# A written TensorE order with overlapping groups, and SiLU as one ScalarE function, in the state space stage of an encoder trunk

## The chip, the cores and the metric

The kernel runs on one core of a Trainium2 chip. The metric is the device time of one execution in microseconds. The kernel before takes 2204.69 us, the median of 3 runs (2203.37 to 2206.54).

## What is computed

Two layers of an encoder trunk, with 512 tokens of width 1024 and 256 memory tokens. Each layer feeds x into three branches: a bidirectional state space branch (SSD), differential attention and cross-attention. Each branch is projected back to 1024 channels and multiplied by a sigmoid gate computed from x; the sum goes through one output projection, the residual and a layer norm. The change is in the SSD branch, of which this is the reference, cut to what matters:

```python
xbc = silu(centred_dwconv(xbc, conv_w, conv_b))      # 5 taps over tokens
xs, bm, cm = split(xbc)       # 32 heads x 64, and 4 groups x 128 for B and for C
dt = softplus(dt_raw + dt_bias); a = -exp(a_log)
y  = scan(xs*dt_f, dt_f*a_f, bm, cm) + flip(scan(flip(...)))  # chunks of 128 tokens
y  = (y + d_skip*xs) * silu(z)
return rmsnorm(y, norm_w)
...
# in scan(): what is within a chunk, and what comes from other chunks
decay  = exp(where(lower, a_cum[q] - a_cum[s], -inf))
y_diag = einsum(cm, bm, decay, xs)
states = einsum(bm, exp(a_cum[-1] - a_cum), xs)       # summed on from chunk to chunk
y_off  = einsum(cm, prev_states, exp(a_cum))
```

## The kernel before: tiles, stages and what sets the order

**Units.** The weights are cut into 336 units of 128x1024 numbers (512 KB). SyncE loads a unit into `wr` (2 buffers), ScalarE copies it rounded to `wh` (3 buffers), and VectorE forms the remainder `wl = wr - wh` (3 buffers). A projection (`proj`, line 166) goes through the 8 slices k of x and makes three matmuls for each, `wl·xh`, `wh·xl`, `wh·xh`: 24 matmuls of 128x512 into one PSUM bank of the pool `pj` (3 banks). The pool `pm` (4 banks) takes the scan's matmuls and `pt` (1 bank) the transposes. `proj2` (line 189) is the same projection as a generator that hands control back after 4 of the 8 slices; before, only the differential attention (`diff`, line 826) uses it.

**The plan.** `T(fn, unit)` (line 128) puts a step on a list. `emit` (line 131) goes through the list, issues the load and the split of units up to two ahead (`look_raw=2, look=2`), and calls the step. A scheduler then places each engine's instructions by priority, which follows the order in which they were issued; `late(n)` (line 100) lowers the priority of what is issued in it, and inside `manual_schedule(engines={PE})` the TensorE order is the written one.

**The SSD stage** (`ssd`, line 446) runs per layer over 4 groups g, each of 4 blocks b of 128 channels (2 heads). In order: `bpart` (457) projects B, runs `conv` (433) and transposes it to `bT`; `cpart` (468) does C and the product of B and C within chunks (`gs`); `dt_tables` (350), in group 0 only, loads `wdt` into the scratch tile `yh`, projects dt, and writes the cumulative sums to DRAM (`dab`, `deb`). In layer 0 the first B and C run side by side (`bcpart`, 482). Then 4 times `xpart` (488: projection, `conv`, four transposes under `late(LX)`, and the copy to `xsT`), `states` (499: for each direction three `xw` on VectorE, each with one matmul into `pm`), and 4 times `zpart` (523) and `ypart` (532). `ypart` loads `eb` and `ab` from `deb` and `dab`, makes two groups of three "far" matmuls, multiplies them into `eb` on VectorE, puts 8 Exp of 128x128 per head over `ab` on ScalarE, forms the two tiles `m` on VectorE, and makes 16 "near" matmuls of `m` and `xsT`; a chain on VectorE and ScalarE then forms `y`, `yh` and `yl`. The output projections `wpart` (589) of group g-1 stand between the `xpart` steps of group g.

**At the end of the stage** come three gate units of branch 0 (`gpart`, 624), the four `wpart` of group 3, and then alternately a gate unit and a `fin` (629), which scales one slice of the branch's output by the norm and the gate. Eight gates of branch 2 are computed in the stage at the places of the table `AHEAD` (line 40) and stored to DRAM (`dgt`, `gate_ahead` at 683).

**SiLU** is x·sigmoid(x) = (x/2)(tanh(x/2)+1). `conv` uses weights halved in advance (`hcw`), so that `acc` holds half of x: ScalarE makes the first tap, VectorE four more (`scalar_tensor_tensor` from PSUM), ScalarE `th = Tanh(acc)`, VectorE `(th+1)*acc`. `zpart` makes `th = Tanh(ps/2)` on ScalarE and `(th+1)*ps` on VectorE. The norm of the branch takes up the factor 2 of z with 4·EPS in place of EPS.

Of the kernel before, what the change touches and what calls it, by code (L numbers as in the profile page):

```python
# [37 lines left out]


AHEAD = {(0, 1): [(2, 0)], (0, 2): [(2, 1)], (0, 3): [(2, 2)], (1, 0): [(2, 3)], (1, 2): [(2, 4)],  # L40
         (2, 0): [(2, 5)], (2, 2): [(2, 6)], (3, 1): [(2, 7)]}
# [14 lines left out]
class Net:  # L56
# [243 lines left out]
    def layer_params(self, l):  # L300
        nc, a = self.nc, self.a
        pr = self.t(self.cp, [P, NP_], "pr", bufs=2)
        nc.sync.dma_start(out=pr, in_=a["pk"][l])
        self.par = pr
        self.hgb = self.t(self.cp, [P, 24], "hgb", bufs=2)
        self.ts(self.hgb, pr[:, PGB:PGB + 24], 0.5, ALU.mult)
        self.hcw = self.t(self.cp, [P, 144], "hcw", bufs=2)
        self.ts(self.hcw, pr[:, PCW:PCW + 144], 0.5, ALU.mult)
# [41 lines left out]
    def dt_tables(self, l):  # L350
# [20 lines left out]
        N = 256  # L371
        ps = self.bank(self.pj, "pj")
# [3 lines left out]
        self.act(xc, ps[:64])  # L376
        pt = self.bank(self.pt, "pt")
# [26 lines left out]
        dtot = self.dtot = self.t(sp, [P, 4, 64], "dtot")  # L404
        pc = self.bank(self.pm, "pm")
        pv = pc.rearrange("p (d c h) -> p d c h", d=4, c=4)
        for d, tri in ((0, self.tf), (1, self.tb)):
            self.mm(pv[:, d], tri, da[:, :, d * 32:(d + 1) * 32])
            self.act(cum[:, :, d * 32:(d + 1) * 32], pv[:, d])
        for d in range(2):  # L410
            self.mm(pv[:, 2 + d], self.ones, da[:, :, d * 32:(d + 1) * 32])
# [9 lines left out]
        self.tt(bi, bi, cum, ALU.subtract)  # L421
        pt = self.bank(self.pt, "pt")
# [10 lines left out]
    def conv(self, ps, ci, out):  # L433
# [9 lines left out]
        self.act(th, acc, AF.Tanh)  # L443
        self.stt(out, th, 1.0, acc, ALU.add, ALU.mult)

    def ssd(self, l):
# [9 lines left out]

        def bpart(g, ps=None):
            def f(wh, wl):
                self.bC = self.t(self.sp, [P, S], "bC")
                self.conv(self.proj(wh, wl) if ps is None else ps, 16 + g, self.bC)  # L460
                pt = self.bank(self.pt, "pt")
                for c in range(4):
                    self.tr(pt[:, c * P:(c + 1) * P], self.bC[:, c * P:(c + 1) * P])
                self.bT = self.t(self.sp, [P, S], "bT")
                self.act(self.bT, pt)
            return f

        def cpart(g, ps=None):
            def f(wh, wl):
                self.cC = self.t(self.sp, [P, S], "cC", bufs=2)  # L470
                self.conv(self.proj(wh, wl) if ps is None else ps, 20 + g, self.cC)
                pg = self.bank(self.pm, "pm")
                for c in range(4):
                    q = slice(c * P, (c + 1) * P)
                    self.mm(pg[:, q], self.bC[:, q], self.cC[:, q])
                self.gs = self.t(self.sp, [P, 4, P], "gs", bufs=2)
                self.act(self.gs, pg.rearrange("p (c q) -> p c q", c=4))
                self.xsT = self.t(self.sp, [P, 4, S], "xsT", bufs=2)
                self.xsC = {}
            return f  # L480

        def bcpart(g):
            def f(*ws):
                for part, w, ps in zip((bpart, cpart), ws, self.proj_side(*ws)):
                    part(g, ps)(*w)
            return f

        def xpart(g, b):
            def f(wh, wl):
                xc = self.xsC[b] = self.t(self.sp, [P, S], f"xsC{b}")  # L490
                self.conv(self.proj(wh, wl), 4 * g + b, xc)
                pt = self.bank(self.pt, "pt")
                with self.late(LX):
                    for c in range(4):
                        self.tr(pt[:, c * P:(c + 1) * P], xc[:, c * P:(c + 1) * P])
                self.act(self.xsT[:, :, b * P:(b + 1) * P], pt.rearrange("p (c e) -> p c e", c=4))
            return f

        def states(g):
            def f():  # L500
                sp = self.sp
                self.prev = {}
                for d, order in ((0, (0, 1, 2)), (1, (3, 2, 1))):
                    hs = slice(d * 32 + g * 8, d * 32 + g * 8 + 8)
                    old = None
                    for c in order:
                        xw = self.t(sp, [P, 8, 64], "xw", bufs=2)
                        self.tt(xw, self.xsT[:, c, :].rearrange("p (h e) -> p h e", h=8),
                                bc(self.wst[:, c, hs, None], [P, 8, 64]), ALU.mult)
                        ps = self.bank(self.pm, "pm")  # L510
                        self.mm(ps, self.bT[:, c * P:(c + 1) * P], xw)
                        pv = self.t(sp, [P, 8, 64], f"prev{d}{c}")
                        psv = ps.rearrange("p (h e) -> p h e", h=8)
                        if old is None:
                            self.act(pv, psv)
                        else:
                            self.tt(pv, old, bc(self.dtot[:, c, hs, None], [P, 8, 64]), ALU.mult)
                            self.tt(pv, pv, psv, ALU.add)
                        old = pv
                        self.prev[d, c + 1 if d == 0 else c - 1] = pv.rearrange("p h e -> p (h e)")  # L520
            return f
# [10 lines left out]
        def ypart(g, b):  # L532
            def f():
                sp = self.sp
                if b == 0:
                    self.yh = self.t(sp, [P, 4, S], "yh", F32R)
                    self.yl = self.t(sp, [P, 4, S], "yl", F32R)

                eb = self.t(sp, [P, 2, S], "eb", bufs=2)
                for hh in range(2):  # L540
                    h = g * 8 + 2 * b + hh
                    src = self.deb.rearrange("(d h) q -> h d q", d=2)[h:h + 1]
                    nc.sync.dma_start(out=eb[hh * 64:(hh + 1) * 64], in_=src.broadcast_to([64, 2, S]))
                for d, cs in ((0, (1, 2, 3)), (1, (0, 1, 2))):
                    ps = self.bank(self.pm, "pm")
                    for c in cs:
                        q = slice(c * P, (c + 1) * P)
                        self.mm(ps[:, q], self.prev[d, c][:, b * P:(b + 1) * P], self.cC[:, q])
                    q = slice(cs[0] * P, (cs[2] + 1) * P)
                    self.tt(eb[:, d, q], ps[:, q], eb[:, d, q], ALU.mult)  # L550

                py = self.bank(self.pm, "pm")
                ms = []
                for hh in range(2):
                    h = g * 8 + 2 * b + hh
                    ab = self.t(sp, [P, 2, 4, P], "ab", bufs=2)
                    src = self.dab.rearrange("(d h) q -> h d q", d=2)[h:h + 1]
                    nc.sync.dma_start(out=ab.rearrange("p d c q -> p d (c q)"), in_=src.broadcast_to([P, 2, S]))

                    self.tt(ab, ab, bc(self.msk[:, :, None, :], [P, 2, 4, P]), ALU.min)  # L560
                    for d in range(2):
                        for c in range(4):
                            j = 32 * d + h
                            self.act(ab[:, d, c, :], ab[:, d, c, :], AF.Exp, bias=self.bias[:, c, j:j + 1])
                    self.tt(ab[:, 0], ab[:, 0], ab[:, 1], ALU.add)
                    m = self.t(sp, [P, 4, P], "m", bufs=3)
                    self.tt(m, ab[:, 0], self.gs, ALU.mult)
                    ms.append(m)
                with self.tc.manual_schedule(engines={mybir.EngineType.PE}):
                    for i in range(8):  # L570
                        c, hh = i // 2, 1 - i % 2
# [741 lines left out]
```

## Time and profile before

| what | value |
|---|---|
| median of 3 runs | 2204.69 us |
| the profiled execution's own time | 2203.02 us |
| its span in the trace | 2201.2 us |
| mean granted TensorE clock | 0.996 |
| TensorE (PE) busy | 2157.3 us, 98% of the span |
| TensorE weight load (PEld) busy | 1779.0 us, 81% |
| VectorE (DVE) busy | 1610.1 us, 73% |
| ScalarE (ACT) busy | 1022.8 us, 46% |
| GpSimd (POOL) busy | 51.2 us, 2% |
| moved by DMA | 295.27 MB, mean 134 GB/s |

The trace counts from the start of the span. Matmuls are pipelined and their ends are modelled, so a row's duration is longer than the step from one matmul to the next. A row of the timeline has start, duration, engine, line, operation, output <- inputs, shapes and count; in brackets the idle time of the engine just before it and what ended that. In the rows by group, the count (x) is followed by the sum in us, the mean in ns, and the idle time before the rows with its releasers. SPq is SyncE's DMA queue.

In the trace the SSD stage of layer 0 fills the stretch from 6 to 507 us and that of layer 1 from 1151 to 1646 us; in between and behind lie cross-attention, differential attention and the output projection of the two layers.

### The profile page before, as it was taken

The page shows a single profiled execution, that of the slowest core. Times are in us where ns is not written, and L with a number is a line of the kernel's source. Part 1 is how long each engine was busy: PE and PEld are TensorE (multiplying, and loading weights), DVE is VectorE, ACT ScalarE, POOL GpSimd, SP SyncE. Part 2 cuts the span into 40 slices and gives each one's busy share as a digit, 9 for nine tenths or more (in the row PEclk, how much of TensorE's full clock was granted, in tenths as well). Part 3 has the DMA queues.
Part 4 walks back from the last instruction along what each step waited for, and adds up shares of the span by engine and source line. Part 5 has one row for each costly group of instructions (what it writes and reads, how often), then busy time and mean ns, then how long its engine had stood idle before and what let it go on. Part 6 is the DMA issues. An engine that isn't in the chain of part 4 may idle for free.

```text
span 2201.2 us, 29202 instructions
## 1 busy us (share of the span) xinstructions
PE 2157.3 (98%) x11122; PEld 1779.0 (81%) x11122; DVE 1610.1 (73%) x2486; ACT 1022.8 (46%) x1935; POOL 51.2 (2%) x38
## 2 busy tenths in 40 slices
PE   8999999999999999999999999999999999999998
PEld 6677877788888888887887777778788888888876
DVE  6797979767554787876567988888854547888667
ACT  4564545433442455553345564555423325555430
POOL 0000000000000000000000000000000000000000
PEclk9999999999999999999999999999999999999999
DMA  4553545435554433325564655444434334333253
GB/s 143 166 168 121 159 125 161 121 95 167 167 163 122 138 112 106 111 82 155 156 208 119 191 145 147 135 145 142 119 107 128 111 112 130 111 110 106 92 158 110
DMA packets 109680, 295.27 MB, mean 134 GB/s; under 512 B 12460, under 2 KB 13028, under 8 KB 109284
## 3 DMA queue, kind: packets, MB, share of 16 engines
q1 hardware_dynamic: 109540, 293.41, 44.5%
q8 instruction: 87, 1.43, 0.3%
q14 instruction: 53, 0.43, 0.1%
HBM read 255.06 MB, written 17.33 MB: 124 GB/s over the span
## 4 chain that ended last, share of the span: by engine, by line
PE 76%; DVE 12%; DMA 8%; ACT 3%; issue 2%; SPq 0%; DVEq 0%; ACTq 0%
PE pj L103 58%; PE pm L103 14%; DMA ab<-dab 5%; PE pt L111 2%; DVE ab L81 2%; DVE wl L81 2%; DVE acc L84 2%; DVE y L81 1%; DMA wr<-wu 1%; DVE yl L84 1%; ACT wh L91 1%; ACT ab L91 1%; DVE m L81 1%; DMA fth<-rd 1%; DVE y L84 1%
## 5 line engine op out<-in xcount | busy, mean ns | idle before, releaser
L103 PE MATMUL pj<-xh,wl 128*128 128x512 f32 x1664 | 664.2, 399 | 5.9 <-ACT mrg L91 3.6
L103 PE MATMUL pj<-xh,wh 128*128 128x512 f32 x1664 | 660.0, 397 | 7.2 <-ACT xh L91 6.0
L103 PE MATMUL pj<-xl,wh 128*128 128x512 f32 x1664 | 660.1, 397 | 0.0
L81 DVE TENSOR_TENSOR wl<-wr,wh 128x1024 fp32r<-128x1024 f32 x330 | 407.0, 1234 | 107.7 <-ACT wh L91 106.9
L91 ACT ACTIVATE wh<-wr 128x1024 fp32r<-128x1024 f32 x330 | 347.4, 1054 | 212.5 <-PE pj L103 130.1
L103 PEld LDWEIGHTS pj<-xh,wh 128*128 128x128 f32 x1664 | 314.0, 189 | 79.5 <-ACT xh L91 6.0
L103 PEld LDWEIGHTS pj<-xh,wl 128*128 128x128 f32 x1664 | 313.9, 189 | 77.4 <-ACT mrg L91 5.3
L103 PEld LDWEIGHTS pj<-xl,wh 128*128 128x128 f32 x1664 | 314.3, 189 | 66.5 <-issue 4.5
L91 ACT ACTIVATE ab<-ab,bias 128x128 f32<-128x128 f32 x512 | 160.8, 392 | 118.4 <-DVE ab L81 117.1
L84 DVE SCALAR_TENSOR_TENSOR acc<-pj,hcw,acc 128x510 f32<-128x510 f32 (+1 forms) x192 | 141.7, 742 | 27.3 <-ACT acc L91 26.3
L941 DVE TENSOR_REDUCE fmx<-pm 128x1 f32<-128x512 f32 x128 | 85.0, 686 | 47.6 <-PE pm L103 47.6
L103 PE MATMUL pj<-dy,wh 128*128 128x512 f32 (+1 forms) x384 | 102.6, 356 | 2.0 <-DVE dy L81 2.0
L103 PE MATMUL pj<-yl,wh 128*128 128x512 f32 x256 | 102.6, 401 | 1.3 <-DVE yl L84 1.2
L103 PE MATMUL pj<-yh,wh 128*128 128x512 f32 x256 | 103.1, 403 | 0.0
L91 ACT ACTIVATE fpp<-pm,fmx 128x512 f32<-128x512 f32 x128 | 87.2, 686 | 33.6 <-DVE fmx L941 33.6
L81 DVE TENSOR_TENSOR ab<-ab,cst 128x1024 f32<-128x1024 f32 x64 | 84.5, 1320 | 24.4 <-DMA ab<-dab 23.8
L103 PE MATMUL pj<-yh,wl 128*128 128x512 f32 x256 | 102.1, 400 | 0.1
L103 PEld LDWEIGHTS pj<-dy,wh 128*128 128x128 f32 x384 | 67.5, 188 | 14.3 <-DVE dy L81 3.2
L103 PE MATMUL pj<-cy,wh 128*128 128x512 f32 x256 | 78.8, 389 | 0.0
L103 PE MATMUL pj<-wh,xl 128*128 128x256 f32 x256 | 73.3, 286 | 0.0
L103 PE MATMUL pj<-wl,xh 128*128 128x256 f32 x256 | 72.4, 283 | 0.0
L103 PE MATMUL pj<-wh,xh 128*128 128x256 f32 x256 | 72.4, 283 | 0.0
(280 smaller groups left out, 3310.7 us busy)
## 6 DMA issues: line engine op xcount, KB each, us to landing
wr<-wu SPq DMA_DIRECT2D x336, 512.0 KB, 3.7
ab<-dab SPq DMA_DIRECT2D x64, 512.0 KB, 5.4
eb<-deb SPq DMA_DIRECT2D x64, 256.0 KB, 4.8
mkv<-dkv SPq DMA_DIRECT2D x16, 512.0 KB, 4.3
rsw<-rx SPq DMA_DIRECT2D x64, 128.0 KB, 2.3
dy<-dy SPq DMA_DIRECT2D x32, 256.0 KB, 2.3
dgt<-tg SPq DMA_DIRECT2D x16, 256.0 KB, 4.2
dkv<-mo SPq DMA_DIRECT2D x16, 256.0 KB, 4.3
```

What stands on the lines that cost most here:

```text
L81: (eng or self.nc.vector).tensor_tensor(out=out, in0=a, in1=b, op=op)
L84: self.nc.vector.scalar_tensor_tensor(out=out, in0=a, scalar=s, in1=b, op0=op0, op1=op1)
L91: self.nc.scalar.activation(out=out, in_=a, func=f, **kw)
L103: self.nc.tensor.matmul(out=out, lhsT=a, rhs=b, start=first, stop=last)
L111: self.nc.tensor.transpose(out=out, in_=x, identity=self.ident)
L941: nc.vector.tensor_reduce(out=mx[:, c:c + 1], in_=ps, axis=AX.X, op=ALU.min)
```

## The change

**SiLU.** In `conv` and `zpart`, ScalarE's activation computes Silu directly; the tiles `th`, the VectorE instruction behind each Tanh and the halved weights `hcw` are gone, and the norm takes EPS. Silu and Exp are in different function tables on ScalarE: the built program has 107 `ACT_TABLE_LOAD` instructions on ScalarE, where the program before has 7. VectorE loses 80 `scalar_tensor_tensor` of 128x512 (48 behind `conv`, 32 behind z) and 2 small ones; no other kind of VectorE instruction changes in number.

**Order.** The whole SSD stage stands in one `manual_schedule` for TensorE. `U(unit, jobs)` puts a unit on the list and the named jobs amid it, after 4 of its 8 slices; `J(fn)` puts a job alone. All projections of the stage go through `proj2`. The old parts are cut smaller: `bturn`, `within`, `xturn` (the transposes and products that stood in `bpart`, `cpart`, `xpart`), `states(g, part)` with one step of both directions at a time, `expos` (the loads, Exp and `m` of a block), `block` (the far matmuls, the near matmuls, then all multiplies), `norm` and `norm_spread`, and `dt_tables` as a generator in five steps. TensorE executes 10,564 instructions before and after.

**Overlap.** The blocks of group g-1 stand between the projections of group g, and so do its z units; `wpart(g-1)` stands behind the `xu` units of group g, two of its PSUM banks at a time. Gate units serve as filling: the 8 of branch 2 and the first 4 of branch 0 are computed in the stage and stored to DRAM; gates 4 to 7 of branch 0 stand between the blocks of group 3; all 8 `fin` follow the last unit of the stage, where before the gate units stood between them. There are 8 more stores to `dgt` and 8 more loads from it.

The diff, cut to its core:

```diff
-AHEAD = {(0, 1): [(2, 0)], (0, 2): [(2, 1)], (0, 3): [(2, 2)], (1, 0): [(2, 3)], (1, 2): [(2, 4)],
...
     def conv(self, ps, ci, out):
-        th = self.t(sp, [P, S], "th", bufs=2)
-        cw = lambda j: self.hcw[:, ci * 5 + j:ci * 5 + j + 1]
-        self.act(acc, ps, AF.Identity, scale=cw(2), bias=self.hcw[:, 120 + ci:121 + ci])
+        cw = lambda j: self.par[:, PCW + ci * 5 + j:PCW + ci * 5 + j + 1]
+        self.act(acc, ps, AF.Identity, scale=cw(2), bias=self.par[:, PCB + ci:PCB + ci + 1])
...
-        self.act(th, acc, AF.Tanh)
-        self.stt(out, th, 1.0, acc, ALU.add, ALU.mult)
+        self.act(out, acc, AF.Silu)
...
+        def xturn(g, b):
+            pt, xc = self.bank(self.pt, "pt"), B["xsC", g, b]
+            for c in range(4):
+                self.tr(pt[:, c * P:(c + 1) * P], xc[:, c * P:(c + 1) * P])
+            self.act(G["xsT", g][:, :, b * P:(b + 1) * P], pt.rearrange("p (c e) -> p c e", c=4))
...
         def zpart(g, b):
             def f(wh, wl):
-                ps = self.proj(wh, wl)
-                th = self.t(self.sp, [P, S], "th", bufs=2)
-                self.act(th, ps, AF.Tanh, scale=0.5)
-                self.sz = self.t(self.sp, [P, S], "sz", bufs=2)
-                self.stt(self.sz, th, 1.0, ps, ALU.add, ALU.mult)
+                ps = yield from self.proj2(wh, wl)
+                sz = B["sz", g, b] = self.t(self.sp, [P, S], "sz", bufs=2)
+                self.act(sz, ps, AF.Silu)
...
+        def gate(i, j, t=None):
+            def f(wh, wl):
+                ps = yield from self.proj2(wh, wl)
+                o = self.t(self.sp, [P, S], "tg", bufs=2) if t is None else t()
+                self.act(o, ps, AF.Tanh, scale=0.5, bias=self.hgb[:, 8 * i + j:8 * i + j + 1])
+                if t is None:
+                    d = self.dgt[i, j] = self.t(self.dp, [P, S], f"dgt{i}{j}")
+                    nc.sync.dma_start(out=d, in_=o)
...
+        early = [gate(2, j) for j in range(KC)] + [gate(0, j) for j in range(4)]
+        def U(unit, *amid):
+            gen, u = unit
+            def f(wh, wl):
+                g = gen(wh, wl)
+                next(g, None)
+                for fn, *args in amid:
+                    fn(*args)
+                next(g, None)
+            self.T(f, u)
...
+        J(lambda: next(tables[0]))
+        if l == 0:
+            self.T(bcpart(0), [(l, UB), (l, UC)])
...
+        J(lambda: next(tables[0]))
+        if l == 0:
+            U(gu(), (lambda: next(tables[0]),))
+            U(xu(0, 0))
...
+        U(gu(), (xturn, 0, 2))
+        J(lambda: next(tables[0], None))
+        U(gu())
+        J(xturn, 0, 3)
+        J(expos, 0, 0)
+        U(gu())
+        J(states, 0, 0)
+        U(zu(0, 0), (states, 0, 1))
+        for g in range(1, 4):
+            p = g - 1
+            U(bu(g))
...
+            U(cu(g))
+            U(gu())
+            J(block, p, 1)
+            U(xu(g, 0), (bturn, g))
+            J(expos, p, 2)
+            U(zu(p, 2), (within, g))
+            U(xu(g, 1))
+            J(block, p, 2)
+            J(xturn, g, 0)
+            U(zu(p, 3))
+            J(expos, p, 3)
+            U(xu(g, 2))
+            J(xturn, g, 1)
+            J(block, p, 3)
+            U(xu(g, 3))
+            U(gu(), (xturn, g, 2))
+            U(wu(p, 0))
+            J(xturn, g, 3)
+            U(wu(p, 1))
+            U(wu(p, 2), (states, g, 0))
+            J(states, g, 1)
+            U(wu(p, 3))
+            J(states, g, 2)
+            J(expos, g, 0)
+            U(zu(g, 0))
+        for b in range(4):
+            U(gate(0, 4 + b, place(4 + b)))
+            J(block, 3, b)
+            if b < 3:
+                U(zu(3, b + 1))
+                J(expos, 3, b + 1)
+        for j in range(4):
+            J(fetch, j)
+        U(wu(3, 0))
+        J(norm)
+        U(wu(3, 1))
+        U(wu(3, 2))
+        J(norm_spread)
+        U(wu(3, 3))
         for j in range(KC):
-            if j + 3 < KC:
-                self.T(gpart(j + 3), (l, UGL + j + 3))
-            self.T(fin(j))
+            J(fin, j)
```

Two places show what moves. On TensorE, at the first states of layer 0 (`xw` is the weighted x of one chunk, `xsC` the convolved block whose transposes go into the bank `pt`, `pj` a projection with weights `wh`, `wl`), there stands before:

```order
L103 MATMUL pj_757<-xh_82,wh_557 128x512
L111 MATMUL pt_509<-cst_81,xsC_84_474 128x128 x4
L103 MATMUL pj_757<-xh_82,wl_558 128x512
L103 MATMUL pj_757<-xl_83,wh_557 128x512
L103 MATMUL pj_757<-xh_82,wh_557 128x512
L103 MATMUL pj_757<-xh_82,wl_558 128x512
L103 MATMUL pj_757<-xl_83,wh_557 128x512
L103 MATMUL pj_757<-xh_82,wh_557 128x512
L103 MATMUL pj_757<-xh_82,wl_558 128x512
L103 MATMUL pm_517<-xw_515,bT_204 128x512
L103 MATMUL pm_523<-xw_521,bT_204 128x512
```

And on TensorE at the same place after the change, where the rows left out are 20 more matmuls of the unit `pj_715`:

```order
L99 MATMUL pj_643<-xh_82,wh_547 128x512
L107 MATMUL pt_672<-cst_81,xsC_92_576 128x128 x4
L99 MATMUL pj_715<-xh_82,wl_587 128x512
L99 MATMUL pj_715<-xl_83,wh_586 128x512
...
L99 MATMUL pj_715<-xl_83,wh_586 128x512
L99 MATMUL pj_715<-xh_82,wh_586 128x512
L99 MATMUL pm_746<-xw_744,bT_378 128x512
L99 MATMUL pm_752<-xw_750,bT_378 128x512
L99 MATMUL pj_762<-xh_82,wl_640 128x512
```

Before, 7 matmuls of a z unit stand between the last transposes and the first matmul that reads `xw`; after, the 24 matmuls of a whole gate unit.

On ScalarE, around the last convolved block of group 1 in layer 0 (`acc` is the convolution's sum, `ab` the Exp of a head, `mrg` the branch's output, `tg` a gate), there stands before:

```order
L91 ACTIVATE acc_1422<-pj_1397,hcw_131 128x512
L91 ACTIVATE wh_1439<-wr_1437 128x1024
L91 ACTIVATE xsT_1146<-pt_1350 128x4x128
L91 ACTIVATE ab_1791<-ab_1791,bias_358 128x128 x4
L91 ACTIVATE mrg_133<-pj_1443 128x512
L91 ACTIVATE ab_1791<-ab_1791,bias_358 128x128 x3
L91 ACTIVATE th_1423<-acc_1422 128x512
L91 ACTIVATE mrg_133<-pj_1457 128x512
L91 ACTIVATE wh_1513<-wr_1511 128x1024
L91 ACTIVATE xsT_1146<-pt_1431 128x4x128
```

And on ScalarE after the change, at the block of the same group:

```order
L87 ACTIVATE xsT_989<-pt_1438 128x4x128
L87 ACTIVATE tg_1456<-pj_1425,hgb_129 128x512
L87 ACTIVATE wh_1462<-wr_1460 128x1024
L87 ACT_TABLE_LOAD
L87 ACTIVATE ab_1659<-ab_1659,bias_541 128x128
L87 ACT_TABLE_LOAD
L87 ACTIVATE xsC_241_1411<-acc_1412 128x512
L87 ACTIVATE mrg_131<-pj_1466 128x512
L87 ACTIVATE mrg_131<-pj_1467 128x512
L87 ACTIVATE xsT_989<-pt_1494 128x4x128
```

Before, seven Exp of a head `ab` and a Tanh stand there with no table load between them; after, one Exp stands ahead of the Silu that makes `xsC`, with a load on each side of it, and the transposes into `pt_1494` wait for that Silu.

More of the change, by code (lines that the diff above doesn't have):

```diff
@@ L371, in dt_tables @@
         N = 256
+        yield
         ps = self.bank(self.pj, "pj")
@@ L488, in xpart @@
         def xpart(g, b):
             def f(wh, wl):
[L490 to L496, printed above, removed]
-            return f
@@ L499, in states @@
[L499 to L521, printed above, removed]
@@ L638, in close @@
             self.sp_ctx.close()
[L640 to L641 removed]
+        self.ahead_gates = {(2, j) for j in range(KC)}
         self.dgt = {}
[L643 to L663 removed]
@@ new lines, in J, with bu, cu, xu @@
+        def J(fn, *args):
+            self.T(lambda: fn(*args))
+        def bu(g):
+            return bpart(g), (l, UB + g)
+        def cu(g):
+            return cpart(g), (l, UC + g)
+        def xu(g, b):
+            return xpart(g, b), (l, UXS + 4 * g + b)
+        def zu(g, b):
+            return zpart(g, b), (l, UZ + 4 * g + b)
+        def wu(g, u):
+            return wpart(g, u), (l, UBS + 4 * g + u)
+        def gu():
+            return early.pop(0)
+        self.T(begin)
+        order = ExitStack()
@@ new lines, in ssd @@
+        self.T(lambda: order.enter_context(self.tc.manual_schedule(engines={mybir.EngineType.PE})))
+        tables = []
+        J(lambda: tables.append(self.dt_tables(l)))
+        J(lambda: next(tables[0]))
+        if l == 0:
+            self.T(bcpart(0), [(l, UB), (l, UC)])
+        else:
+            U(bu(0))
+            U(cu(0))
+            U(gu())
[3 more added lines that the diff above has]
+            U(xu(0, 0))
+        else:
+            U(xu(0, 0), (lambda: next(tables[0]),))
@@ new lines, in ssd @@
+        U(gu(), (bturn, 0))
+        U(xu(0, 1), (within, 0))
+        J(xturn, 0, 0)
+        U(xu(0, 2))
+        U(gu())
+        J(xturn, 0, 1)
+        J(lambda: next(tables[0]))
+        U(xu(0, 3))
+        U(gu(), (xturn, 0, 2))
[3 more added lines that the diff above has]
+        J(expos, 0, 0)
+        U(gu())
+        J(states, 0, 0)
[3 more added lines that the diff above has]
+            U(bu(g))
+            if g == 1:
+                J(states, 0, 2)
+                U(zu(p, 1), (block, p, 0))
+            else:
+                J(block, p, 0)
+                U(zu(p, 1))
+            J(expos, p, 1)
+            U(cu(g))
+            U(gu())
+            J(block, p, 1)
[21 more added lines that the diff above has]
+            U(zu(g, 0))
@@ L675, in ssd @@
+        self.T(order.close)
         self.T(close)
```

282 lines of the change are left out of this document (147 added, 135 removed).

## The prediction

> **What bounds the kernel now.** I read the busy times first.
>
> ```profile
> PE 2157.3 (98%) x11122; PEld 1779.0 (81%) x11122; DVE 1610.1 (73%) x2486; ACT 1022.8 (46%) x1935; POOL 51.2 (2%) x38
> ```
>
> TensorE is busy for 98% of the span. The change leaves its work as it is (10,564 instructions both times), so only the gaps in its work can be won, and only in the two stages that are edited. The view by windows has these stages (6 to 507 and 1151 to 1646 us) and, from a second call, two short stretches in layer 0; its columns are the window, its length, the busy time of PE, PEld, DVE, ACT and POOL with counts, the granted clock, the DMA share and GB/s.
>
> ```profile
> 6.00:507.00 501.00, 489.26 (x2392) 386.70 (x2393) 400.56 (x559) 251.29 (x503) 25.30 (x17) 0.99 0.47 138
> 1151.00:1646.00 495.00, 486.55 (x2428) 386.39 (x2428) 399.34 (x552) 248.61 (x500) 25.21 (x16) 1.00 0.48 138
> 70.00:82.00 12.00, 8.62 (x22) 4.61 (x21) 7.73 (x12) 5.17 (x12) 0.00 (x0) 0.86 0.77 175
> 100.00:112.00 12.00, 9.97 (x55) 8.33 (x54) 10.04 (x15) 6.32 (x19) 1.49 (x1) 0.86 0.42 128
> ```
>
> In 996 us of the two stages VectorE is busy for 800 (80%) and ScalarE for 500 (50%). What TensorE waits for in each stage is the next view (total, times, longest; layer 0 first).
>
> ```profile
> PE pj L103 <- ACT xh L91: 6.0, 1, 6.0
> PE pm L103 <- DVE m L81: 3.4, 3, 2.0
> PE pm L103 <- DVE xw L81: 3.4, 1, 3.4
> PE pj L103 <- ACT mrg L91: 1.5, 2, 1.3
> PE pj L103 <- ACT wh L91: 1.2, 1, 1.2
> PE pt L111 <- DVE bC L84: 0.9, 1, 0.9
> PE pm L103 <- DVE cC L84: 0.5, 1, 0.5
> PE pj L103 <- DVE yl L84: 0.4, 2, 0.2
> ```
>
> ```profile
> PE pm L103 <- DVE m L81: 3.0, 4, 1.2
> PE pj L103 <- ACT mrg L91: 2.1, 2, 1.8
> PE pt L111 <- DVE bC L84: 2.0, 2, 1.5
> PE pj L103 <- DVE yl L84: 0.7, 3, 0.3
> PE pm L103 <- DVE cC L84: 0.4, 1, 0.4
> ```
>
> The 6.0 us is the start of the kernel and stays. The others make 11.3 us in layer 0 and 8.2 us in layer 1. Two of them have an echo, which the timeline places:
>
> ```profile
> 75.72 2.08 PE L103 MATMUL pm<-xw,bT 128*128 128x512 f32 x2 [3.38 <-DVE xw L81]
> 105.52 1.26 PE L103 MATMUL pm<-m,xsT 128*64 128x128 f32 x16 [2.03 <-DVE m L81]
> ```
>
> These fall in the two short stretches with a clock of 0.86: 0.14 x 12 us = 1.7 us lost in each beside the wait. **At stake: 11.3 + 8.2 + 3.4 = 22.9 us**, 1% of the time. [...]
>
> **What the order removes.** The step from matmul to matmul comes from a full stretch:
>
> ```profile
> 252.69 0.39 PE L103 MATMUL pj<-xh,wl 128*128 128x512 f32 x1
> ...
> 254.05 0.39 PE L103 MATMUL pj<-xh,wl 128*128 128x512 f32 x1
> ```
>
> Six steps take 1.36 us, so one takes 0.227 and a unit of 24 takes 5.45 us. Before the first states there stand 7 matmuls (1.6 us) behind the last transposes, and afterwards a whole unit, 3.9 us more cover against a wait of 3.38. The products of B and C, and the transposes of B, get a unit or more behind their convolution; the near matmuls get the far ones and the units since `expos`. So each of the 19.5 us of waits has a cover that exceeds it, and with the waits go the two clock losses. I take all 22.9 as removed, and set against it what stays or comes.
>
> **What the Silu moves.** These rows by group carry the durations.
>
> ```profile
> L91 ACT ACT_TABLE_LOAD x7 | 9.0, 1283 | 0.8 <-PEq L1304 0.7
> L91 ACT ACTIVATE ab<-ab,bias 128x128 f32<-128x128 f32 x512 | 160.8, 392 | 118.4 <-DVE ab L81 117.1 <-ACT sz L91 1.4
> L91 ACT ACTIVATE th<-acc 128x512 f32<-128x512 f32 x48 | 30.2, 629 | 39.9 <-DVE acc L84 39.7
> L91 ACT ACTIVATE tg<-pj,hgb 128x512 f32<-128x512 f32 x16 | 10.9, 682 | 40.6 <-PE pj L103 40.6
> L91 ACT ACTIVATE wh<-wr 128x1024 fp32r<-128x1024 f32 x330 | 347.4, 1054 | 212.5 <-PE pj L103 130.1 <-DMA wr<-wu 45.7 <-PE pm L103 28.0
> L91 ACT ACTIVATE yh<-y,pr 128x512 fp32r<-128x512 f32 x32 | 23.1, 721 | 52.1 <-DVE y L81 52.0
> L91 ACT ACTIVATE acc<-pj,hcw 128x512 f32<-128x512 f32 x48 | 37.0, 772 | 28.1 <-PE pj L103 23.3 <-issue 3.2 <-DVE bC L84 1.1
> L84 DVE SCALAR_TENSOR_TENSOR acc<-pj,hcw,acc 128x510 f32<-128x510 f32 (+1 forms) x192 | 141.7, 742 | 27.3 <-ACT acc L91 26.3
> L84 DVE SCALAR_TENSOR_TENSOR xsC<-th,acc 128x512 f32<-128x512 f32 x32 | 22.0, 687 | 4.0 <-ACT th L91 4.0
> L81 DVE TENSOR_TENSOR y<-y,eb 128x384 f32<-128x384 f32 x64 | 35.1, 549 | 0.1
> L84 DVE SCALAR_TENSOR_TENSOR y<-xsC,pr,pm 128x512 f32<-128x512 f32 x32 | 23.7, 741 | 1.3 <-PE pm L103 0.8
> L81 DVE TENSOR_TENSOR y<-y,sz 128x512 f32<-128x512 f32 x32 | 21.9, 684 | 0.1
> L84 DVE SCALAR_TENSOR_TENSOR yl<-y,pr,yh 128x512 fp32r<-128x512 f32 x32 | 34.3, 1072 | 1.6 <-ACT yh L91 1.6
> ```
>
> VectorE loses 80 instructions of 0.687 us: 55 us, so that it is busy for 745 of 996 us (75%). ScalarE gains 100 loads of 1.283: 128 us, so that it is busy for 628 of 996 (63%). No run shows a Silu; I take the Tanh's 0.629, the nearest row. Both engines remain below TensorE, so the sums alone cost nothing, and the path counts only where a chain through them is longer than the matmuls that cover it.
>
> What a switch costs beyond its load row, the trace shows at one place on ScalarE:
>
> ```profile
> 59.83 1.28 ACT L91 ACT_TABLE_LOAD   x1
> 61.12 0.63 ACT L91 ACTIVATE th<-acc 128x512 f32<-128x512 f32 x1
> ```
>
> The next instruction starts 0.01 us after the load. I take 1.283 per switch. [...]
>
> **What stays or comes.**
>
> 1. The start of layer 0. The dt projection now stands right behind B and C, and its copy stands on ScalarE behind both convolutions: 0.772 + 8 x 0.742 + 0.629 = 7.3 us, or 8.6 with a load. TensorE has 24 matmuls of dt and 12 of the gate unit amid which the transposes of dt stand: 36 x 0.227 = 8.2; with the copy's some 0.6 us the chain is 0.3 short or 1.0 long. I take 1.0, from 0 to 2.
> 2. The end of each stage. Behind the last near matmuls the chain to `yl` is 0.741 + 2 x 0.549 + 0.684 + 0.721 + 1.072 = 4.3 us, up to 5.4 with the two multiplies of `eb` ahead. The first `wpart` of group 3 has 18 matmuls ahead of the slice that needs it: 4.1 us. That leaves 0.2 to 1.3; a split of a unit in between would add 1.2. I take 1.0 per layer: 2.0.
> 3. The tight place, the last transposes of groups 1 to 3. From the end of the gate unit ScalarE does the gate, a split, a load, an Exp, a load and the Silu: 0.682 + 1.054 + 1.283 + 0.392 + 1.283 + 0.629 = 5.32 us, against 5.45 for the `wpart` unit that covers it. With hand-overs this is 0 to 1 each; I take 0.4, six times: 2.4.
> 4. The border to cross-attention. Eight `fin` with 16 VectorE instructions (16 x 0.687 = 11.0 us) now stand behind the last unit, where before gate units lay between them, while the two units loaded ahead cover 10.9 us. 0 to 4; I take 2.0 once.
> 5. Late VectorE. Of the waits above 14.7 us are on VectorE (`m`, `xw`, `bC`, `cC`, `yl`), which stays 75% busy. I leave 2.0, from 0 to 4.
>
> The 8 more stores and loads of gates are on SyncE, 0.25 MB each, none followed by a reader within a unit: nothing. If they pushed a weight load late, the buffers two units ahead (10.9 us) would have to be used up first.
>
> **The sum.** 22.9 - (1.0 + 2.0 + 2.4 + 2.0 + 2.0) = 13.5 us won. 2203.0 - 13.5 = 2189.5 for a profiled execution, which stands 1.7 below the median of the runs: **2191 us**. About 0.2% (4.4 us) is what a measurement of this kernel can tell from no change.
>
> **Rivals.**
>
> (a) All gaps go, and one more with them: just behind layer 0's stage there is this wait for a split.
>
> ```profile
> 532.10 0.50 PE L103 MATMUL pj<-xh,wl 128*128 128x512 f32 x1 [2.20 <-DVE wl L81]
> ```
>
> If VectorE, with 55 us less to do, is in time there, that is 2.2 and a clock loss like the two above, 1.7. Gain 22.9 + 3.9 = 26.8: 2178. Against it speaks item 4. Chance 0.15.
>
> (b) VectorE remains the bound of the stage: 75% instead of 80% is little, and the order is only as good as its latest operand. Then half of the 14.7 us of waits stay, in place of item 5: 13.5 + 2.0 - 7.4 = 8.1 won, about 2197; with a quarter of them 2193, with three quarters 2200. Chance 0.15, of which 0.04 is within 0.2%.
>
> (c) A switch costs more than its row, up to a second load's time. The tight place then takes 5.32 + 2 x 1.283 = 7.9 us against 5.45: 2.4 each, 14.7 in all instead of 2.4, and 1.2 of the gain is left: about 2203.5, no change. The row at 61.12 is against it. Chance 0.07. [...]
>
> (d) Slower: ScalarE in order. The Silu now stands on ScalarE behind an Exp whose input comes from a DMA, and the transposes of that block, with TensorE's fixed order behind them, wait for it. VectorE's wait for that DMA in layer 0 is in the trace:
>
> ```profile
> DVE ab L81 <- DMA ab<-dab: 14.0, 12, 3.7
> ```
>
> The mean is 14.0/12 = 1.17 us. If it came through at each of the 32 transposed blocks, that is 37 us: 2203.0 - 13.5 + 37.3 + 1.7, about 2229. It decides from 13.5/32 = 0.42 us a block. For it: no scheduler moves a ready unit ahead any more. Against it: `expos` is issued a unit or more ahead of `block`, and most blocks have a unit between convolution and transposes. Chance 0.13.
>
> **How the numbers follow.** My forecast has 0.50. Faster by over 0.2%: 0.50 + 0.15 + 0.11 = 0.76. Within 0.2%: 0.04 + 0.07 = 0.11. Slower: 0.13. The range is 2178 to 2211: below it lies half of (a), above it most of (d), together under 0.2; its upper end is (d) at half of its price, 2191 + 19, rounded up. The forecast's own range goes from items 1 to 5 at their lower ends (0 + 0.4 + 0 + 0 + 0, so 22.5 won: 2182) to half way from the values taken to the upper ends (2 + 5 + 6 + 4 + 4 = 21; half way from 9.4 is 15.2, so 7.7 won: 2197).
>
> **What would show it.** Right: in the two stages TensorE's idle time falls from 20 us to under 10; no gap of 2 us or more; `ACT_TABLE_LOAD` x107 at 1.28 us; granted clock 1.00 where 0.86 stood; waits on `xw`, `m`, `bC` gone, with small ones on `yl` and `xsC` instead. Wrong: waits of 1 us or more on `xsC` in every group with Exp or loads ahead of it ((c) or (d)), waits on `m` or `wl` as before ((b)), or a busy time of TensorE that differs by more than 10 us from 2157, which would mean that its work or clock moved and not its gaps.

## The result and the profile after

The changed kernel takes 2189.86 us, the median of 6 runs (2188.43 to 2191.16), beside 2204.52 for the kernel before (6 runs, 2202.09 to 2207.53): 0.9932 of it, 95% interval 0.992 to 0.9944. The forecast was 2191. The profiled execution took 2190.09 us with a span of 2188.3, 12.9 us less than before. The busy times of the page:

```profile
PE 2148.1 (98%) x11122; PEld 1787.3 (82%) x11122; DVE 1546.6 (71%) x2404; ACT 1152.1 (53%) x2035; POOL 61.3 (3%) x38
```

VectorE is down by 63.5 us and ScalarE up by 129.3. TensorE is busy 9.2 us less with the same 11,122 matmul records, so most of the gain is not in what the trace calls idle; that comes back below. The two stages (now 6 to 503 and 1140 to 1640 us) and two short stretches by windows, with the columns of the prediction's fence:

```profile
6.00:503.00 497.00, 488.17 (x2412) 394.16 (x2413) 368.49 (x515) 316.02 (x554) 30.57 (x17) 1.00 0.51 146
1140.00:1640.00 500.00, 492.30 (x2465) 398.47 (x2466) 369.60 (x515) 317.65 (x556) 30.57 (x17) 1.00 0.51 145
170.00:182.00 12.00, 8.17 (x31) 6.33 (x30) 12.00 (x17) 9.63 (x16) 1.31 (x1) 0.86 0.50 142
1306.00:1318.00 12.00, 9.22 (x36) 7.21 (x35) 12.00 (x17) 9.65 (x18) 1.31 (x1) 0.86 0.48 133
```

TensorE still stands idle for 8.8 and 7.7 us in the stages, where 11.7 and 8.5 had been. The clock has moved its 0.86 to two new places. What TensorE waits for in layer 0, and then in layer 1:

```profile
PE pj L99 <- ACT xh L87: 6.0, 1, 6.0
PE pt L107 <- ACT xsC L87: 5.3, 3, 3.8
PE pj L99 <- ACT wh L87: 2.1, 1, 2.1
PE pm L99 <- DVE prev L77: 0.8, 1, 0.8
PE pm L99 <- DVE m L77: 0.6, 1, 0.6
```

```profile
PE pt L107 <- ACT xsC L87: 4.1, 4, 2.8
PE pj L99 <- DVE wl L77: 1.1, 2, 0.9
PE pm L99 <- DVE m L77: 1.0, 1, 1.0
PE pm L99 <- DVE prev L77: 0.8, 1, 0.8
```

(Two rows of layer 1 are left out behind these, 0.7 us at its border and 0.5 on `mrg`.) Against the rows of before: `xw`, `bC`, `cC`, `yl` and `mrg<-ACT` are gone, `m` fell from 6.4 to 1.6 us, and a row that was not there has come, 9.4 us on `xsC`: the transposes wait for a convolved block.

By stretches that begin and end at the same work in both traces, layer 0's stage became 7.5 us shorter. Layer 1's stage with its cross-attention, taken together since some matmuls moved over the border between them, became 3.8 shorter. The rest is 1.7 us shorter behind the stages of layer 1 and 0.2 longer in layer 0. So the time was won where the change is.

**The new wait, step by step.** The longest `xsC` wait in TensorE's timeline stands ahead of the third transposes of group 1:

```profile
174.21 0.66 PE L107 MATMUL pt<-cst,xsC 128*128 128x128 f32 x4 [3.83 <-ACT xsC L87]
```

ScalarE's timeline just before it names the Silu that it waited for:

```profile
168.00 1.28 ACT L87 ACT_TABLE_LOAD   x1 [4.77 <-DVE ab L77]
169.29 2.45 ACT L87 ACTIVATE ab<-ab,bias 128x128 f32<-128x128 f32 x8
172.23 1.28 ACT L87 ACT_TABLE_LOAD   x1 [0.48 <-DVE acc L80]
173.52 0.63 ACT L87 ACTIVATE xsC<-acc 128x512 f32<-128x512 f32 x1
```

The Exp are done at 171.7, but the Silu's input comes only at 172.2 from VectorE, which had stood still itself:

```profile
159.55 1.29 DVE L77 TENSOR_TENSOR m<-ab,gs 128x512 f32<-128x512 f32 x2
...
166.71 1.23 DVE L77 TENSOR_TENSOR ab<-ab,cst 128x1024 f32<-128x1024 f32 x1 [4.73 <-DMA ab<-dab]
...
171.41 0.74 DVE L80 SCALAR_TENSOR_TENSOR acc<-pj,pr,acc 128x510 f32<-128x510 f32 x1
```

The masking of `ab` waits 4.73 us for its DMA, and the four taps of the convolution are queued behind it. SyncE had issued that DMA only when one of the two `ab` tiles came free, behind the first of the two `m` at 159.55, which read them:

```profile
160.30 0.38 SPq L551 DMA_DIRECT2D ab<-dab  x1
```

So this reading was put to the test: the chain is buffer of `ab`, DMA, masking, convolution, Silu, transposes. The load at 172.23 stands in it as well, with its 1.28 us, since here it starts only 0.08 us behind the last tap (171.41 + 0.74), which makes the Silu's input.

### The profile page after: what moved, and what is told of

Same layout as the page of the kernel before. It is cut to its first block, busy times and chain, and to the rows that moved or that the text cites. A ratio compares the mean times of both kernels' runs of the same rounds, so it can differ in the third digit from the quotient of the medians.

```text
span 2188.3 us, 29240 instructions
## 1 busy us (share of the span) xinstructions
PE 2148.1 (98%) x11122; PEld 1787.3 (82%) x11122; DVE 1546.6 (71%) x2404; ACT 1152.1 (53%) x2035; POOL 61.3 (3%) x38
## 4 chain that ended last, share of the span: by engine, by line
PE 78%; DVE 9%; DMA 7%; ACT 2%; issue 2%; SPq 0%; DVEq 0%; ACTq 0%
PE pj L99 61%; PE pm L99 14%; DMA ab<-dab 4%; PE pt L107 2%; DVE acc L80 2%; DVE wl L77 2%; DMA wr<-wu 2%; DVE y L77 1%; DMA fth<-rd 1%; DVE eb L77 1%; ACT wh L87 1%; DVE ab L77 1%; ACT L87 1%; DVE y L80 1%; DMA mkv<-dkv 0%
## 5 line engine op out<-in xcount | busy, mean ns | idle before, releaser
L99 PE MATMUL pj<-xh,wh 128*128 128x512 f32 x1664 | 652.5, 393 | 8.1 <-ACT xh L87 6.0
L99 PE MATMUL pj<-xl,wh 128*128 128x512 f32 x1664 | 652.0, 392 | 0.0
L87 ACT ACT_TABLE_LOAD x107 | 137.3, 1283 | 93.4 <-DVE ab L77 31.7
L80 DVE SCALAR_TENSOR_TENSOR acc<-pj,pr,acc 128x510 f32<-128x510 f32 (+1 forms) x192 | 142.2, 744 | 32.6 <-ACT acc L87 31.7
L77 DVE TENSOR_TENSOR ab<-ab,cst 128x1024 f32<-128x1024 f32 x64 | 78.2, 1223 | 72.9 <-DMA ab<-dab 72.8
L77 POOL TENSOR_TENSOR sqa<-sqa,sz 128x512 f32<-128x512 f32 x32 | 60.1, 1878 | 887.6 <-ACT sz L87 887.6
```

The lines of the kernel that those rows point to most:

```text
L77: (eng or self.nc.vector).tensor_tensor(out=out, in0=a, in1=b, op=op)
L80: self.nc.vector.scalar_tensor_tensor(out=out, in0=a, scalar=s, in1=b, op0=op0, op1=op1)
L87: self.nc.scalar.activation(out=out, in_=a, func=f, **kw)
L99: self.nc.tensor.matmul(out=out, lhsT=a, rhs=b, start=first, stop=last)
```

## The experiments

The theory after the result: the new order removes VectorE's old waits, and what is left is the DMA of `ab`, which has two buffers. Rivals: the gain is VectorE's 55 us and not the order's; the `xsC` wait is the table loads; the gain is TensorE changing less often between projection matmuls and others, since before many transposes stood alone among them. Each ratio is to the kernel before, timed along with it, with its 95% interval.

**The order alone.** The changed kernel with SiLU as before:

```diff
-        self.act(out, acc, AF.Silu)
+        self.act(th, acc, AF.Tanh)
+        self.stt(out, th, 1.0, acc, ALU.add, ALU.mult)
```

(also for z, with the halved weights and 4·EPS).

> The changed kernel with SiLU as before (halved weights, Tanh on ScalarE and the multiply on VectorE): the new order alone, with 7 table loads instead of 107. If the gain is the order's (waits on VectorE covered, TensorE changing less often between projection and other matmuls), it is between 2181 and 2190 us: no later than the changed kernel, and up to 9 us earlier if the 9.4 us that TensorE now waits for xsC come from the table loads. If the gain is the 55 us that VectorE no longer works, it goes back to 2197 or more, with the waits on m, xw and bC as before. If the waits for xsC come from VectorE standing at the masking of ab for a late DMA, they stay at 8 to 10 us here too, since that has nothing to do with the tables.

Measured 0.9963 (0.995 to 0.9976), 2192.85 beside 2201.03 us: 8 us of the gain without Silu. Its largest waits over the whole span, in the view by what TensorE waits for:

```profile
PE pt L107 <- DVE xsC L80: 6.7, 4, 2.8
...
PE pm L99 <- DVE xw L77: 4.4, 5, 1.5
```

The order alone pays, about half. The other half came with Silu, but the intervals of the two kernels all but touch, and three buffers will leave no difference (below). The waits for `xsC` stay with 7 table loads, so most of them are not the tables'; at 6.7 us they are somewhat under my 8 to 10, and the longest is 2.8 in place of 3.8. `xw` is a wait again: with VectorE's multiplies back, it is late there.

**Silu alone, in the old order.** The kernel before with Silu in `conv` and `zpart` and EPS, nothing else.

> The kernel before with SiLU as one ScalarE function and nothing else changed: 119 table loads in the old order. If VectorE's load is what made TensorE wait, the 55 us less give most of the gain: 2192 to 2196 us. If the order is what counts, 2201 to 2208: the same waits on m, xw, bC. [...]

Measured 1.0098 (1.0082 to 1.0114): 2221.89 beside 2201.03, 21 us slower, which neither branch reached. ScalarE was the one waited for, but the rows show no price of a switch beyond its load: the Silu at 240.29 below starts 0.02 us behind the end of the load. One row carries most of the loss:

```profile
PE pt L111 <- ACT bC L91: 15.4, 4, 4.2
```

ScalarE at one of these four places:

```profile
237.71 1.26 ACT L91 ACTIVATE ab<-ab,bias 128x128 f32<-128x128 f32 x4
238.99 1.28 ACT L91 ACT_TABLE_LOAD   x1
240.29 0.63 ACT L91 ACTIVATE bC<-acc 128x512 f32<-128x512 f32 x1
```

The Silu of B stands behind Exp and a load, and the transposes of B, only a few matmuls behind its projection in the old order, wait for it. TensorE's clock is at half speed in five stretches, one of them of 6.8 us. So what Silu is worth depends on the order around it: minus 21 us in the old one with two buffers of `ab`.

**Three buffers of ab.** One edit to the changed kernel:

```diff
-                ab = self.t(sp, [P, 2, 4, P], "ab", bufs=2)
+                ab = self.t(sp, [P, 2, 4, P], "ab", bufs=3)
```

> The changed kernel with three buffers of ab instead of two, so that the DMA of the next head can start before the last but one is used up. If the waits for xsC come from VectorE standing at the masking of ab (4.7 us idle at 162 us) ahead of the convolution, they fall from 9.4 us to under 3, the two stretches of half clock behind the 3.8 and 2.8 us waits go (1.7 us each), and the time is 2178 to 2183 us. If they come from the table loads ahead of the Silu, they stay and the time is 2189 to 2191.

Measured 0.9875 (0.986 to 0.9889), 2173.02 beside 2201.03; once more, as an anchor:

> The changed kernel with three buffers of ab once more, as the anchor of this comparison: 0.986 to 0.989 of the kernel before.

Measured 0.9868 (0.9853 to 0.9883), 2172.57 beside 2201.1. The changed kernel, as the anchor of the second comparison:

> The changed kernel once more, as the anchor for the other kernels of this comparison. 0.992 to 0.994 of the kernel before.

Measured 0.9937 (0.9923 to 0.995), 2189.41 beside 2203.31. So a third buffer is worth another 0.6%, somewhat more than expected, and this version beats both kernels. TensorE's waits over the whole span with three buffers, the first and the fifth row:

```profile
PE pj L99 <- ACT xh L87: 6.0, 1, 6.0
...
PE pm L99 <- DVE prev L77: 1.5, 2, 0.8
```

`xsC` is gone from the head of the view (0.65 us are left). VectorE's wait for the DMA in layer 0, with two buffers and with three:

```profile
DVE ab L77 <- DMA ab<-dab: 36.3, 22, 4.9
```

```profile
DVE ab L77 <- DMA ab<-dab: 19.8, 12, 4.2
```

It was 14.0 us in the kernel before. The new order had made this wait longer. With three buffers more than half of it is still there, but it no longer comes through to the transposes.

**Three buffers, and SiLU as before.** Tanh and the multiply in place, for want of room for `th`.

> The changed kernel with three buffers of ab, and SiLU as before (Tanh, then the multiply on VectorE in place): 7 table loads. If Silu pays by the 55 us that VectorE no longer works, the waits for xw, prev and xsC come back in part and it is 5 to 9 us slower than with Silu and three buffers, about 0.990 to 0.992 of before. If the late DMA of ab was all that stood in the way, both forms of SiLU give the same now: 0.987 to 0.988. If the table loads cost something at the last transposes of a group (1.28 against 0.69 us of a multiply), it is faster: 0.985.

Measured 0.9871 (0.9858 to 0.9885): no difference from Silu with three buffers. My first reason, that VectorE's 55 us would come back as waits, is wrong here: its page has VectorE busy for 1600.6 us, 57 more than with Silu, and of the waits on `xw` and `xsC` only 0.4 us. The 92 more table loads of the Silu version (118 us of ScalarE) cost nothing either.

**The old order with three buffers**, with Silu and with Tanh in place (in both, two gates at a time use the tile `tg`, to make room).

> The kernel before with Silu and three buffers of ab (two gates at a time use another tile, to make room). The old order with Silu lost 20 us, 15.4 of it in waits for bC, which stands on ScalarE behind Exp and table loads. If the Exp ahead of it are late because of the DMA of ab, most of this goes: 0.99 to 1.00 of before. If the loads and the Exp themselves are what bC waits for, it stays at 1.005 to 1.01.

Measured 0.9983 (0.9975 to 0.9992): the loss of 21 us is gone, all but 0.8 us of `bC` with it, and 7.0 us on `m` and 5.8 on `mrg` are at the head. VectorE's wait for the DMA of `ab` in layer 0 fell from 25.1 us to 6.4. So in the old order too the Exp that stand ahead of the Silu were late by that DMA.

> The kernel before with three buffers of ab and nothing else (SiLU by Tanh, multiplied in place; two gates at a time use another tile). VectorE's wait for ab (14.0 us in layer 0) goes. If that wait is also what made m, xw and bC late in the old order, 6.4 + 3.4 + 2.9 us of TensorE's waits and the echoes go: 2188 to 2192, 0.993 to 0.995. If the old order is late for want of cover, no change: 0.999 to 1.001.

Measured 1.003 (1.002 to 1.0041), 6 us slower, which neither branch had. The premise of both did not come about: VectorE's wait for `ab` in layer 0 stayed where it was, at 15.2 us for 14.0, and TensorE's waits over the whole span on `wl` rose from 3.1 us to 9.7 and those on `bC` from 2.9:

```profile
DVE ab L81 <- DMA ab<-dab: 15.2, 9, 3.7
```

```profile
PE pt L111 <- DVE bC L84: 11.6, 7, 2.5
```

So this run does not show what an earlier `ab` is worth in the old order with Tanh. Why the scheduler's order gets worse with a third buffer, and whether the tile `tg` or the multiply in place has a part in it, was not tried.

| order | SiLU | two buffers of ab | three |
|---|---|---|---|
| old | Tanh | 1 | 1.003 |
| old | Silu | 1.0098 | 0.9983 |
| new | Tanh | 0.9963 | 0.9871 |
| new | Silu | 0.9932, 0.9937 | 0.9875, 0.9868 |

**Transposes one by one.** In the changed kernel, and then with three buffers:

```diff
-            for c in range(4):
-                self.tr(pt[:, c * P:(c + 1) * P], xc[:, c * P:(c + 1) * P])
...
+            one(0)
+            self.lone = [lambda c=c: one(c) for c in (1, 2, 3)]
...
+            if self.lone:
+                self.lone.pop(0)()
```

> The changed kernel with the four transposes of each convolved block taken apart: the first where it was, the others one by one behind the next three slices of the following unit. No wait is added but on the copy behind them, which has over 10 us in most places. If a change of TensorE between projection matmuls and others has a price of its own (by the steps in the trace before, a chain of four lone transposes takes about 0.56 us beside the projection's steps, four together 0.46), the 32 chains make it 3 us slower, about 2193 us, with no new wait. If only gaps count, no change: 2190 us.

Measured 0.9971 (0.9962 to 0.9981), 2195.27 beside 2201.03: 0.0034 above the changed kernel of the second comparison, some 7 us, but with new waits (4.0 us on `xw`, 3.1 on `xsT`), so that it tells nothing on the price. The steps in its trace do: four lone transposes cost 0.476 us beside the projection's steps, four together 0.454. My estimate of 0.56 had counted the tail of the last one, which four together have as well. This concerns the transposes alone: the matmuls of the states, and the far and near matmuls of a block, also stood apart at places of the old order, and no run put those apart.

> The kernel with three buffers of ab, with the transposes of a convolved block one by one between the slices of the next unit. Without waits in the way this shows the price of a change of TensorE between projection and other matmuls. By the steps in the run with lone transposes (four lone ones cost 0.476 us beside the projection's, four together 0.454) it is 0.7 us in all: no difference that can be told. If the first estimate held (0.56 against 0.46), 3 us slower. If xw again comes late because the last transposes end later, there are waits on xw and xsT and 4 to 6 us.

Measured 0.9943 (0.9931 to 0.9956), 2189.09: 16 us slower than with four together, against at most 6 expected.

```profile
PE pm L99 <- DVE xw L77: 6.5, 3, 3.9
...
PE pt L107 <- ACT xsT L87: 3.1, 2, 1.6
```

With 2.8 us on `xsC` these are 12.4 us of waits, where the anchor has 0.6 of this kind, and there are two stretches of half clock (3.4), one of them at the border of layer 1, where nothing was changed. Together they make up most of the 16. So the time is in the main that of late readers; what is left for the lone transposes is 1 to 2 us, less than two profiles of one kernel differ by. The branch with late readers had the right mechanism, and came to 16 us in place of 4 to 6.

**The first states without their cover**, with three buffers:

```diff
         J(xturn, 0, 3)
-        J(expos, 0, 0)
-        U(gu())
         J(states, 0, 0)
+        J(expos, 0, 0)
+        U(gu())
```

> The kernel with three buffers of ab, with the first states moved ahead of the gate unit that stands between them and the last transposes of group 0, once per layer. If cover is counted as I counted it (chain of the trace before: 1.6 us of matmuls plus the wait of 3.38), TensorE waits 5 us for xw in each layer, with half clock behind: 2 x 6.7 = 13 us slower, 2186. If most of that wait was VectorE's queue, which the new order leaves shorter at this place, only the chain itself is left: transposes done at 82.3, xw ready at 83.9 us in the trace with three buffers, 1.5 us in each layer, and it is 3 us slower: 2176.

Measured 0.9891 (0.9877 to 0.9904), 2177.49: 4.9 us slower than the anchor with three buffers.

```profile
PE pm L99 <- DVE xw L77: 3.1, 2, 1.6
...
PE pt L107 <- ACT xsC L87: 2.9, 2, 1.9
```

1.5 us a layer, as the chain from transposes to `xw` says, and not the 5 that I had put on this place from the trace before. That trace has no wait at this place. TensorE's first matmuls with `xw` start there without one, and the wait of 3.38 us, at 75.72 us, belongs to the next step of the states:

```profile
69.04 1.92 PE L103 MATMUL pm<-xw,bT 128*128 128x512 f32 x4
```

VectorE's rows show what stood ahead of that next step's `xw`:

```profile
73.24 1.23 DVE L81 TENSOR_TENSOR ab<-ab,cst 128x1024 f32<-128x1024 f32 x1 [3.72 <-DMA ab<-dab]
...
74.98 0.69 DVE L81 TENSOR_TENSOR xw<-xsT,wst 128x512 f32<-128x512 f32 x1
```

So the longest wait within the stages of the old order came from a DMA of `ab` as well, with VectorE idle and not overworked. The unit of cover ahead of the first states is worth some 1.5 us a layer in the new order, and is not what took the 3.38 away.

Beside the 1.5 us there are some 2.3 us more on `xsC` and one stretch of half clock, 1.7; the sum of 7.1 is above the 4.9 of the medians, and single profiles of these kernels differ by as much.

## Why the prediction was right, and where it was not

The time came out at 2189.9 for 2191, and the direction came from the order, as forecast (the order alone gives 8 us, and one unit of cover taken away at two places costs 4.9). That the number came so close is luck. The sum behind it held by errors that cancel, and by a gain that it had put at nothing.

The signs say as much. The loads came as forecast, 107 of 1.28 us. But TensorE's idle time in the two stages fell from 20.2 us to 16.5 and not under 10, there are three waits of over 2 us (3.83, 2.78, and 2.12 at the start), and the clock fell at two new places. TensorE's busy time moved by 9.2 us, just short of the 10 that were to mean that its work or clock moved and not its gaps.

What was at stake. Of the 22.9 us, the waits on `xw`, `bC`, `cC`, `yl` and `mrg` did go. That each wait "has a cover that exceeds it" failed for `m`, which kept 1.6 us, and the wait on `xw` was read at the wrong place: the 7 matmuls of the old order were cover enough for the first states, and the 3.38 us stood one step later, behind a DMA of `ab`.

Item 1, the start: no wait at dt at all, for 1.0; but the second unit's split, whose 1.2 us of before I had taken as removed, now costs 2.1. Item 2, the ends: no wait on `yl`, for 2.0. Item 4, the border: 1.71 us for the 2.20 of before and no half clock behind it, for 2.0 of loss:

```profile
521.28 0.39 PE L99 MATMUL pj<-wl,mhl 128*128 128x256 f32 x1 [1.71 <-DVE wl L77]
```

These three I had sized too large, and of rival (a) the clock's 1.7 us came true. Item 5: 3.1 (`m`, `prev`) for 2.0. Item 3, the tight place, is the one that the trace shows almost word for word. ScalarE in group 2 of layer 0:

```profile
285.33 0.69 ACT L87 ACTIVATE tg<-pj,hgb 128x512 f32<-128x512 f32 x1 [0.80 <-PE pj L99]
285.92 1.05 ACT L87 ACTIVATE wh<-wr 128x1024 fp32r<-128x1024 f32 x1
286.99 1.28 ACT L87 ACT_TABLE_LOAD   x1
289.13 0.40 ACT L87 ACTIVATE ab<-ab,bias 128x128 f32<-128x128 f32 x1 [0.86 <-DVE ab L77]
289.84 1.28 ACT L87 ACT_TABLE_LOAD   x1 [0.30 <-DVE acc L80]
291.13 0.63 ACT L87 ACTIVATE xsC<-acc 128x512 f32<-128x512 f32 x1
```

5.32 us of work and 1.16 of waits for VectorE against the cover of 5.45: TensorE waits 1.08 there, and 0.38 and 0.44 in two other groups, 1.9 in all for 2.4.

The step that failed is the one that gave rival (d) up: "most blocks have a unit between convolution and transposes" is true, and not enough. At the second and third transposes of group 1 an `ab` whose DMA is late stands ahead of the convolution, on VectorE and not on ScalarE as I had it: 3.83 + 2.78 + 0.68 us of waits and twice 1.7 of half clock, 10.7 us that the sum did not have. The rival's mechanism was there at 3 of 32 places; its price of 1.17 us each was a mean over 12 waits of the old trace, the longest of them 3.7.

So the sum as measured, by the rows: 22.9 at stake, and 1.7 + 0.5 at the border, less 2.1 (start), 1.9 (item 3), 3.1 (item 5), 10.7 and 1.0 of small waits (on `mrg`, `wl` and `xsC`): 6.3 us. Outside the stages a wait of cross-attention on a DMA rose from 1.4 us to 3.4, and behind the stages of layer 1 waits on `dy` fell from 1.4 to 0.4; with 0.4 more in two small rows that makes 4.9. The views over the whole span say the same: TensorE's waits come to 27.3 us before and 24.1 after, and there is one stretch of half clock less.

The trace has 12.9. The other 8.0 are not in rows of waits, and here a second step of the prediction failed: "only the gaps in its work can be won". TensorE's busy time fell by 9.2 us, 1.7 of it the clock's, which is the same thing seen from the other side. The waits view counts from the modelled end of the matmul before and leaves short ones out: the 3.38 us of before, for example, were a step of 3.76 from start to start, 0.23 of which a matmul takes in a full stretch.

Counted from start to start, each step of TensorE against the median step of its kind in the trace before, the 8.0 are roughly these: 1 us of such remainders at waits; 2 us of steps between projection matmuls; and 5 us of steps to and from the scan's matmuls and transposes, 3 of them at the blocks, the states and the transposes of x and 1.3 at the products and transposes of B and C. In part these last stood apart before and are together now, and in part they waited for less than the view counts; which part is which stays open. So the trace bears out the covered waits for under half of the gain, and the rival that TensorE changes less often between projection matmuls and others is not excluded for the rest.

Rival (b), VectorE as the bound, is out: 57 us more on VectorE change nothing with three buffers of `ab`. Rival (c) is out: a load's row was its whole price here. The Silu at 291.13 above starts 0.01 us behind its load, and so does the next instruction behind 101 of the 107 loads of this trace (mean 1283 ns); behind the other six ScalarE waits for VectorE's `ab` or a DMA. Silu between Exp costs 21 us in the old order with two buffers. With three buffers the old order with Silu is at 0.9983, beside 1.003 with Tanh, and in the new order 99 loads cost nothing.

## What to carry to other kernels

When an order is written by hand, look for the loads behind it as well: here the new order was held up by a buffer count, and one more tile gave as much again as the whole change. Where a wait is put down to an engine, see whether that engine was working or waiting itself. The sum of an engine's function switches says little: 118 us of loads cost nothing here once the data ahead of them came in time. When a forecast's number comes true, hold its signs against the trace as well. And a wait's length in the old trace can be that of a queue; in a new order, count the chain itself.

## What was not expected of the hardware

The granted clock fell to 0.50 behind gaps of TensorE of 1.9 to 3.8 us: waits of 3.38, 2.03 and 2.20 us before, of 3.83 and 2.78 after, of 1.88 in the run with the bare states. Each time it stayed so for 3.4 us (in the trace after, 0.50 from 175.4 to 178.8 us). With three buffers one run had such a stretch at 1236 us with nothing ahead of it but the two waits on `prev` shown above, 1.5 us together, with 1.25 us from the end of one to the end of the other:

```profile
1232.00:1244.00 12.00, 10.49 (x55) 8.41 (x54) 11.25 (x18) 7.52 (x19) 0.00 (x0) 0.86 0.36 119
```

The second run of the same kernel had none. Length alone does not decide: in the second profile of the changed kernel TensorE waits 3.18 us for `xsC` up to 1308.27 us, longer than most of these, and the clock stays full.

```profile
1302.00:1314.00 12.00, 8.82 (x41) 7.06 (x40) 12.00 (x17) 11.15 (x19) 1.32 (x1) 1.00 0.44 111
```

What length, nearness or moment of gaps decides was not tried. In these runs the clock fell behind single waits down to 1.88 us, and not behind each of them (the 3.18 us above).
